# Issuing the second modulation's products directly behind the first's, and the last rows' squares behind the first features

## The chip, the cores and the metric

The kernel runs on one core of a Trainium2 chip. The metric is the device time of one execution in microseconds, and of a set of executions the median. The engines are named as the profile names them: PE multiplies matrices (PEld is its weight load), DVE and ACT work element by element, POOL is a third such engine, and SP only issues DMA transfers.

## The reference

One layer of a diffusion backbone for 128 context rows and 1024 latent rows of width 1024. What matters here is its head: a conditioning vector gives six modulations, of which the first two (shift and scale) enter the normalised rows ahead of the input projection.

```python
def ada_mods(cond, w_ada_l, b_ada_l):
    m = jax.nn.silu(cond) @ w_ada_l + b_ada_l          # 1024 -> 6 x 1024
    return jnp.split(m.reshape(-1, 1, 6 * D_MODEL), 6, axis=-1)

sh1, sc1, g1, sh2, sc2, g2 = mods
h = rmsnorm(x, norm1_w) * (1 + sc1) + sh1
aq, ak, av, mq, mk, mv, mo, mg = jnp.split(h @ w_in, SPLIT_POINTS, axis=-1)
... # attention head group, mLSTM head group, output projection
x = x + g1 * mix
x = x + g2 * swiglu(rmsnorm(x, norm2_w) * (1 + sc2) + sh2, w_gu, w_down)
```

Context rows use a second conditioning vector, so each modulation is a 1024 x 2 result.

## The kernel before

The 1152 rows are nine blocks of 128, handled in three chunks of three blocks (`x3[c]`, c = 0, 1, 2). The program's first 100 us go through these stages.

1. **Loads.** SP issues the rows of chunks 0 and 1, the four pieces `kraw` of the input projection's key, value and gate columns, then sixteen tiles `ada_w[n][k]` (n = 0 the shift's weights, n = 1 the scale's, eight tiles of 512 KB each; the trace calls them `aw`), and last the rows of chunk 2. After them come the four `iraw` tiles of the query columns and, through `ada_rest`, tiles `a4` (trace: `a`) of the four other modulations; these have three buffers and are asked for again as the products free them.
2. **Rows.** `normalise(c)` squares three blocks on ACT (L355), takes an inverse square root on DVE by a dozen dependent operations on 128x3 numbers (L127 to L133, `rsqrt`), and scales the rows on DVE (L358). `turn(c)` transposes them on PE (L116) into two PSUM banks a block, which ACT (L371) and DVE (L372) copy back.
3. **First two modulations.** `strip_products` (L341) multiplies one weight tile half by the padded silu vector; it uses a 32-column strip of PE, so products with different k run side by side. Of each modulation ACT and DVE copy two `part` tiles (L388) from PSUM, `cols_from_strips` turns them into columns with eight small products (L347), and `modulation` adds the bias on DVE. `kvg.pairs` splits the `kraw` pieces into half-precision pairs on ACT and DVE (L218, L219).
4. **Features.** From both modulations a bound is taken and a power-of-two scale made (L397 to L402, with two small PE products, L116 and L175). `features(c)` then writes each chunk as a high part (ACT, L507) and a low part (DVE, L508 and L137), for eight k tiles.
5. **First projection.** `linear_tok` multiplies chunk by chunk with the key/value/gate pairs, three products for each pair (L483 to L485); ACT (L492, L493) and DVE (L496) take the results out. In chunks 1 and 2 the side work `steps` (absolute maxima of the query weights on ACT, L198, then DVE L200, a PE transpose, DVE L171 and L161 to L164, a PE product L175) and `ada` (the a4 products on PE) is woven in.

The order on each engine is not written out: a scheduler places every instruction by its program position, its dependencies and its priority, and the result is one fixed list for each engine. `hot(n)` raises the priority of what is issued inside it by n. `normalise(2)` stands in the program after the products of chunk 0, and `turn(2)` after those of chunk 1. The rows' results are also taken onward: `norm_rope` normalises and rotates the keys (DVE L666 to L686, POOL L668 and L685) and the new key cache goes out (SP, L694).

## Time and profile before

| | |
|---|---|
| median of 3 runs | 1572.1 us (1570.31 to 1574.45) |
| the profiled execution | 1574.08 us, of which 1572.3 us are its span |
| mean granted clock of PE | 0.979 |
| busy share of the span: PE, DVE, ACT, POOL | 95%, 65%, 49%, 17% |
| chain that ended last: PE, DVE, DMA, ACT | 77%, 11%, 5%, 4% |
| PE busy in the first 20 us, and from 20 to 40, 40 to 60, 60 to 80 | 7.79, 16.64, 15.99, 16.78 us |

A row of a timeline gives the start, the time from the first to the last of the merged instructions, the engine, the line, the operation with its tiles, the number of records, and in brackets how long the engine had been idle and what ended the idle time. PE makes two records of one f32 product with a 512-column output in this trace: sixteen products of a modulation are 32 records. SPq is the queue of SP, where a row is the issue of a DMA and not its transfer.

### The profile page before, as it was taken

The numbers are of one execution on the slowest core, as the hardware profiler recorded it, in microseconds if no ns is written. First come the engines' busy times: TensorE is split into PE (matmuls) and PEld (weight loads), VectorE is DVE, ScalarE is ACT, GpSimd is POOL, SyncE is SP. The second block draws the span as 40 slices with busy tenths as digits, with TensorE's granted clock in tenths as the row PEclk, the third lists the DMA queues.
The fourth block names the chain that finished last, engine by engine and source line by source line (L and its number), as shares of the span: only waits on it lengthen the run. The fifth ranks groups of instructions, "written<-read, shape, count | busy, mean of one in ns | idle before, by whom it ended". The sixth has DMA issues, their size and how long they took to land.

```text
span 1572.3 us, 23397 instructions
## 1 busy us (share of the span) xinstructions
PE 1487.7 (95%) x8539; PEld 1247.3 (79%) x8539; DVE 1022.9 (65%) x2025; ACT 771.8 (49%) x1409; POOL 271.4 (17%) x357
## 2 busy tenths in 40 slices
PE   6899999999999689999999999999999999999996
PEld 3544567676766468898998989989898989999995
DVE  4878554737659576677555677877866585554555
ACT  4754465847656344545432444556552443323332
POOL 0213333322343242100110101000010101001111
PEclk9899999999999799999999999999999999999998
DMA  9664323523556847767555447878763545544441
GB/s 360 186 182 157 97 68 41 121 47 68 114 150 162 265 80 197 184 174 175 154 154 149 147 126 236 195 170 180 179 162 114 168 133 168 161 130 138 143 139 54
DMA packets 387881, 236.91 MB, mean 151 GB/s; under 512 B 170198, under 2 KB 346790, under 8 KB 387766
## 3 DMA queue, kind: packets, MB, share of 16 engines
q1 hardware_dynamic: 385110, 231.84, 54.1%
q10 hardware_dynamic: 2656, 3.58, 1.1%
q8 instruction: 67, 1.10, 0.3%
q14 instruction: 48, 0.39, 0.1%
HBM read 183.79 MB, written 13.26 MB: 125 GB/s over the span
## 4 chain that ended last, share of the span: by engine, by line
PE 77%; DVE 11%; DMA 5%; ACT 4%; issue 2%; SPq 0%; POOL 0%; ACTq 0%; DVEq 0%; POOLq 0%
PE mm L1316 11%; PE mm L1317 11%; PE mm L1315 11%; PE mm L1115 5%; PE mm L1116 5%; PE mm L1117 5%; PE S L1035 3%; PE wi L483 3%; PE wi L485 3%; PE wi L484 3%; PE mm L116 2%; PE mm L1147 1%; PE mm L1148 1%; PE mm L1149 1%; PE po L1060 1%
## 5 line engine op out<-in xcount | busy, mean ns | idle before, releaser
L152 ACT CAST whi<-raw 128x1024 fp32r<-128x1024 f32 (+1 forms) x216 | 222.3, 1029 | 411.0 <-PE mm L1316 156.5
L137 DVE TENSOR_TENSOR wlo<-raw,whi 128x1024 fp32r<-128x1024 f32 (+1 forms) x216 | 260.4, 1206 | 202.9 <-ACT whi L152 202.3
L1316 PE MATMUL mm<-aTl,whi 128*128 128x384 f32 x1056 | 355.7, 337 | 2.7 <-DVE aTl L137 2.7
L1317 PE MATMUL mm<-aTh,wlo 128*128 128x384 f32 x1056 | 354.3, 336 | 0.0
L1315 PE MATMUL mm<-aTh,whi 128*128 128x384 f32 x1056 | 353.3, 336 | 0.0
L137 POOL TENSOR_TENSOR hl<-tn,hl 128x384 fp32r<-128x384 f32 x66 | 84.4, 1279 | 840.0 <-ACT hl L1338 748.3
L1316 PEld LDWEIGHTS mm<-aTl,whi 128*128 128x128 f32 x1056 | 198.5, 188 | 3.9 <-DVE aTl L137 3.3
L1315 PEld LDWEIGHTS mm<-aTh,whi 128*128 128x128 f32 x1056 | 198.1, 188 | 0.6
L1317 PEld LDWEIGHTS mm<-aTh,wlo 128*128 128x128 f32 x1056 | 198.4, 188 | 0.0
L1116 PE MATMUL mm<-wlo,hl 128*128 128x512 f32 x372 | 145.7, 392 | 0.0
L1115 PE MATMUL mm<-whi,hl 128*128 128x512 f32 x372 | 144.3, 392 | 0.0
L1117 PE MATMUL mm<-whi,hl 128*128 128x512 f32 x372 | 143.4, 392 | 0.0
L483 PE MATMUL wi<-ipair,hT 128*128 128x384 f16 (+2 forms) x408 | 135.6, 335 | 1.7 <-ACT hT L507 1.2
L484 PE MATMUL wi<-ipair,hT 128*128 128x384 f16 (+2 forms) x408 | 135.6, 335 | 0.0
L485 PE MATMUL wi<-ipair,hT 128*128 128x384 f16 (+2 forms) x408 | 132.1, 335 | 1.0 <-DVE hT L137 1.0
L1042 DVE SCALAR_TENSOR_TENSOR pl<-pr,st,ph 128x1152 f16<-128x1152 f32 (+1 forms) x72 | 96.0, 1333 | 31.7 <-ACT ph L1041 31.4
L1037 DVE TENSOR_REDUCE st<-S 128x1 f32<-128x1152 f32 (+1 forms) x72 | 88.9, 1235 | 16.3 <-PE S L1035 16.1
L1038 ACT ACTIVATE pr<-S,st 128x1152 f32<-128x1152 f32 (+1 forms) x72 | 81.3, 1130 | 32.4 <-DVE st L1037 29.3
L1041 ACT ACTIVATE ph<-pr,st 128x1152 f16<-128x1152 f32 (+1 forms) x72 | 83.9, 1165 | 23.8 <-DVE st L1040 6.7
L1035 PE MATMUL S<-kst,qT 128*128 128x384 f32 (+1 forms) x400 | 87.6, 349 | 4.8 <-ACT pr L1038 4.8
L1104 DVE TENSOR_TENSOR t<-mm,gl 128x512 f32<-128x512 f32 x102 | 69.1, 687 | 26.2 <-DMA gl<-g_d 11.5
L1117 PEld LDWEIGHTS mm<-whi,hl 128*128 128x128 f32 x372 | 69.9, 188 | 14.2
(375 smaller groups left out, 2538.4 us busy)
## 6 DMA issues: line engine op xcount, KB each, us to landing
raw<-in_w_gu_dram SPq DMA_DIRECT2D x132, 512.0 KB
raw<-in_w_down_dram SPq DMA_DIRECT2D x60, 512.0 KB
a<-in_w_ada_dram SPq DMA_DIRECT2D x24, 512.0 KB
gl<-g_d SPq DMA_DIRECT2D x36, 256.0 KB
aw<-in_w_ada_dram SPq DMA_DIRECT2D x16, 512.0 KB
iraw<-in_w_in_dram SPq DMA_DIRECT2D x32, 256.0 KB
raw<-in_w_out_dram SPq DMA_DIRECT2D x12, 512.0 KB
x<-in_x_sample_dram SPq DMA_DIRECT2D x11, 512.0 KB
```

What stands on the lines that cost most here:

```text
L137: (dve if eng == "dve" else pool).tensor_tensor(out=out, in0=full, in1=hi, op=ALU.subtract)
L152: nc.scalar.copy(hi[:, :n], raw[:, :n])
L483: mm(ps[:, :n], ah, wh[:, k % 2, c0 : c0 + n], start=(k == 0), stop=False)
L484: mm(ps[:, :n], ah, wl[:, k % 2, c0 : c0 + n], start=False, stop=False)
L485: mm(ps[:, :n], al, wh[:, k % 2, c0 : c0 + n], start=False, stop=(k == KD - 1))
L1035: mm(S[:, n, 0:w], qT[:, h, :], kst[kv][:, t, c0 + n * w : c0 + (n + 1) * w], start=(t == 0), stop=(t == 1))
L1115: mm(ps, ah, wh[:, k % 2, :], start=(k == 0), stop=False)
L1116: mm(ps, ah, wl[:, k % 2, :], start=False, stop=False)
L1117: mm(ps, al, wh[:, k % 2, :], start=False, stop=(k == nk - 1))
L1315: mm(ps, wh[:, k, :], th[:, k, :], start=(k == 0), stop=False)
L1316: mm(ps, wh[:, k, :], tl[:, k, :], start=False, stop=False)
L1317: mm(ps, wl[:, k, :], th[:, k, :], start=False, stop=(k == KD - 1))
```

## The change

Two things move, both by order of issue alone. A new construct, `tc.issue_after(instruction)`, holds what is issued inside it behind that instruction in the scheduler's order.

- The four PSUM banks of both modulations are taken at once. All products of modulation 0 come first, then its two `part` copies, and `kvg.pairs` only behind the ACT copy. The products of modulation 1 follow directly: those with k = 0 to 3, then the columns of the shift's first half, the product with k = 4, the columns of its second half, then k = 5 to 7. The scale's columns come last, as before. The columns use banks of the other pool (`bank`), and `part` has four buffers in place of two.
- `features(c)` returns its last ACT instruction. `normalise(2)` is held behind that of `features(0)`, and the products and side work of chunk 1 behind that of `features(1)`.

```diff
-    kvg_pairs = kvg.pairs(1)
-
-    for n, out in ((0, shift1), (1, scale1)):
-        halves = [bankA(), bankA()]
-        for k in range(KD):
-            for j, pe in enumerate(halves):
-                strip_products(pe, k, silp, ada_w[n][k][:, j * 512 : (j + 1) * 512], 2 * j)
-        with hot(300):
-            for j, pe in enumerate(halves):
-                part = p0.tile([P, 512], F32, name=nm("part"), tag="part", bufs=2)
-                (nc.scalar.copy if j == 0 else dve.tensor_copy)(part, pe)
-                cols_from_strips(out, n, j, part, bankA)
+
+    halves = [[bankA(), bankA()] for _ in range(2)]
+
+    def first_products(n, ks):
+        for k in ks:
+            for j, pe in enumerate(halves[n]):
+                last = strip_products(pe, k, silp, ada_w[n][k][:, j * 512 : (j + 1) * 512], 2 * j)
+        return last
+
+    def first_parts(n):
+        parts = [p0.tile([P, 512], F32, name=nm("part"), tag="part", bufs=4) for _ in range(2)]
+        dve.tensor_copy(parts[1], halves[n][1])
+        return parts, nc.scalar.copy(parts[0], halves[n][0]).ins
+
+    first_products(0, range(KD))
+    with hot(300):
+        parts, last = first_parts(0)
+    with tc.issue_after(last):
+        kvg_pairs = kvg.pairs(1)
+    for j, ks in enumerate(((0, 1, 2, 3), (4,))):
+        last = first_products(1, ks).ins
+        with hot(300), tc.issue_after(last):
+            cols_from_strips(shift1, 0, j, parts[j], bank)
+    with hot(300):
+        first_products(1, (5, 6, 7))
+        parts, _ = first_parts(1)
+        for j in range(2):
+            cols_from_strips(scale1, 1, j, parts[j], bank)
...
     for c in range(NCH):
         with hot(100):
-            features(c)
+            last = features(c)
...
         if c > 0:
-            weave(prods, chain(steps, ada), KD, 10)
+            with tc.issue_after(last) if c == 1 else nullcontext():
+                weave(prods, chain(steps, ada), KD, 10)
         else:
             emit(prods)
         if c == 0:
-            normalise(2)
+            with tc.issue_after(last):
+                normalise(2)
```

The first place is PE between the two modulations. `aw_0_7` is the last weight tile of the shift, `aw_1_0` the first and `aw_1_7` the last of the scale; `part` are the copies whose columns L347 makes. Before:

```order
L341 MATMUL wi_366<-aw_0_7_167,silp 32x512
L347 MATMUL wi_385<-strip_sel,part_383 128x2 x4
L347 MATMUL wi_393<-strip_sel,part_391 128x2 x4
L341 MATMUL wi_399<-aw_1_0_169,silp 32x512
L341 MATMUL wi_400<-aw_1_0_169,silp 32x512
L341 MATMUL wi_399<-aw_1_1_171,silp 32x512
```

After, from the fourth tile of the scale on:

```order
L341 MATMUL wi_356<-aw_1_3_175,silp 32x512
L347 MATMUL mm_397<-strip_sel,part_373 128x2 x4
L341 MATMUL wi_355<-aw_1_4_177,silp 32x512
L341 MATMUL wi_356<-aw_1_4_177,silp 32x512
L347 MATMUL mm_405<-strip_sel,part_374 128x2 x4
L341 MATMUL wi_355<-aw_1_5_179,silp 32x512
```

The shift's columns leave the place between the two modulations and stand inside the second one. The last product (`aw_1_7`) and what follows it keep their order.

The second place is DVE behind the features of chunk 1: `hT_440` is their last low part, `ry_627` the inverse square root of chunk 2's rows, `x_2` these rows, `isc_689` and `pv_728` the scale of the query weights, for which PE waits. Before, the operations of the root were spread among the features:

```order
L137 TENSOR_TENSOR hT_440<-full_673,hT_440 128x384
L358 TENSOR_SCALAR x_2_134<-x_2_134,ry_627 128x1024 x3
L200 TENSOR_REDUCE isc_689<-isc_689 128x1
L128 TENSOR_SCALAR rh_1120<-rv_1117 128x2
L129 TENSOR_SCALAR ry_1118<-rh_1120 128x2
L131 TENSOR_TENSOR rt_1119<-ry_1118 128x2
L171 TENSOR_REDUCE pv_728<-mm_726 1x1
```

After, the root begins with the last low part, and the rows `x_2` come out as follows:

```order
L133 TENSOR_SCALAR ry_627<-rt_628,ry_627 128x3
L131 TENSOR_TENSOR rt_1119<-ry_1118 128x2
L358 TENSOR_SCALAR x_2_134<-x_2_134,ry_627 128x1024 x3
L132 TENSOR_SCALAR rt_1119<-rt_1119,rv_1117 128x2
L512 TENSOR_SCALAR G<-mm_677,isc_332,gbias 128x2x4 x2
L512 TENSOR_SCALAR G<-mm_678,isc_332,gbias 128x2x4 x2
L133 TENSOR_SCALAR ry_1118<-rt_1119,ry_1118 128x2
L200 TENSOR_REDUCE isc_689<-isc_689 128x1
L512 TENSOR_SCALAR G<-mm_679,isc_332,gbias 128x2x4 x2
L171 TENSOR_REDUCE pv_728<-mm_726 1x1
L685 TENSOR_REDUCE nrs_1181<-nr_143_1179 128x8
L161 TENSOR_SCALAR pv_728<-pv_728 1x1
```

The twelve steps of the root and its three row scalings now stand in one piece ahead of L200 and L171, and a reduction of 128x512 numbers (L685, before L666) stands between L171 and L161.

The third place is PE in the turn of chunk 2: `mm_802` to `mm_831` are its six transposed half blocks, `a_89` to `a_93` the first four `a4` tiles (three buffers, so `a_93` is loaded into that of `a_89`). Before:

```order
L341 MATMUL mm_770<-a_91_759,silp_473 32x256 x4
L116 MATMUL mm_807<-ident,x_2_134 128x128 x4
L116 MATMUL mm_814<-ident,x_2_134 128x128 x4
L116 MATMUL mm_819<-ident,x_2_134 128x128 x4
L341 MATMUL mm_770<-a_93_784,silp_473 32x256 x4
L116 MATMUL mm_826<-ident,x_2_134 128x128 x4
L116 MATMUL mm_831<-ident,x_2_134 128x128 x4
```

After:

```order
L116 MATMUL mm_814<-ident,x_2_134 128x128 x4
L341 MATMUL mm_770<-a_91_759,silp_473 32x256 x3
L341 MATMUL mm_770<-a_93_784,silp_473 32x256 x3
L116 MATMUL mm_819<-ident,x_2_134 128x128 x4
L341 MATMUL mm_770<-a_93_784,silp_473 32x256
L116 MATMUL mm_826<-ident,x_2_134 128x128 x4
L116 MATMUL mm_831<-ident,x_2_134 128x128 x4
```

The products of `a_93`, and with them the wait for its load, now stand ahead of three half blocks in place of two. On ACT the three squares of chunk 2 (L355) leave the place ahead of the first feature: two now stand directly behind the last feature of chunk 1, the third among the results of chunk 0. On SP the output of the key cache (L694) comes ahead of three `a4` loads instead of behind them, and a query row block (L729) ahead of one later `a4` load. Farther on, a few neighbouring instructions of the attention and mLSTM stages trade places.

More of the change, by code (lines that the diff above doesn't have):

```diff
@@ L1 @@
 import math
-from contextlib import ExitStack
+from contextlib import ExitStack, nullcontext
 import concourse.bass as bass
@@ L340, in strip_products @@
         s = (k + turn) % 4
-        mm(ps[32 * s : 32 * s + 32, :], silp[:, k, :], rows, start=(k < 4), stop=(k >= 4), tile_position=(0, 32 * s))
+        return mm(ps[32 * s : 32 * s + 32, :], silp[:, k, :], rows, start=(k < 4), stop=(k >= 4), tile_position=(0, 32 * s))
     def cols_from_strips(out, n, j, part, new):
@@ L506, in features @@
                 s, t = scale1[:, k, cnd : cnd + 1], shift1[:, k, cnd : cnd + 1]
-                act(hh[:, k, i : i + n], v[:, k, i : i + n], AF.Identity, scale=s, bias=t)
+                last = act(hh[:, k, i : i + n], v[:, k, i : i + n], AF.Identity, scale=s, bias=t)
                 dve.tensor_scalar(out=full[:, i : i + n], in0=v[:, k, i : i + n], scalar1=s, scalar2=t, op0=ALU.mult, op1=ALU.add)
             sub(hl[:, k], full, hh[:, k], "dve")
+        return last.ins
     for c in range(NCH):
         with hot(100):
-            features(c)
+            last = features(c)
         prods = linear_tok(kvg_pairs, 0, 272, evac_kvg, (tuple(range(c * CB, c * CB + CB)),), bank if c == 1 else bankA)
         if c > 0:
-            weave(prods, chain(steps, ada), KD, 10)
+            with tc.issue_after(last) if c == 1 else nullcontext():
+                weave(prods, chain(steps, ada), KD, 10)
         else:
```

## The prediction

> **What bounds the kernel now.** I read the page's shares and its chain first, then the first 140 us engine by engine.

> ```profile
> PE 1487.7 (95%) x8539; PEld 1247.3 (79%) x8539; DVE 1022.9 (65%) x2025; ACT 771.8 (49%) x1409; POOL 271.4 (17%) x357
> PE 77%; DVE 11%; DMA 5%; ACT 4%; issue 2%; SPq 0%; POOL 0%; ACTq 0%; DVEq 0%; POOLq 0%
> ```

> PE is idle for 1572.3 - 1487.7 = 85 us in all, and the change works on the part of that in the head. PE's timeline there:

> ```profile
> 26.45 1.25 PE L341 MATMUL wi<-aw,silp 128*32 128x512 f32 x8
> 29.95 3.57 PE L347 MATMUL wi<-strip_sel,part 128*128 128x2 f32 x16 [2.25 <-ACT part L388]
> 33.45 5.41 PE L341 MATMUL wi<-aw,silp 128*32 128x512 f32 x32
> 39.91 1.95 PE L347 MATMUL wi<-strip_sel,part 128*128 128x2 f32 x16 [1.05 <-ACT part L388]
> ```

> The shift's products end at 27.70. PE waits 2.25 us for a copy that stands behind four pair pieces on ACT, makes columns for 3.5 us, and starts the scale's products at 33.45. They end at 38.86. That gap is what the change fills; what it is worth depends on when the scale's weights land. Three views tell: PE's weight loads (timeline), SP's queue (timeline), and the windows of one microsecond, whose last three columns are the granted clock, the DMA share and GB/s.

> ```profile
> 37.80 0.14 PEld L341 LDWEIGHTS wi<-aw,silp 128*32 128x32 f32 x4 [0.33 <-DMA aw<-in_w_ada_dram]
> ```
> ```profile
> 37.77 0.37 SPq L193 DMA_DIRECT2D iraw<-in_w_in_dram  x1
> ```
> ```profile
> 29.00:30.00 1.00, 0.06 (x1) 0.06 (x1) 1.00 (x3) 0.89 (x2) 0.00 (x0) 0.65 1.02 410
> 35.00:36.00 1.00, 1.00 (x8) 0.19 (x4) 0.00 (x0) 0.00 (x0) 0.00 (x0) 0.50 1.01 401
> 37.00:38.00 1.00, 1.00 (x14) 0.30 (x8) 0.00 (x0) 0.00 (x0) 0.00 (x0) 1.00 1.01 406
> ```

> The last weight tile is already waited for: its weight load at 37.80 was held 0.33 us by the DMA. SP's next query load goes out at 37.77, at the same moment. The DMA engines are full (share 1.0, 400 to 410 GB/s), and 0.524 MB at 406 GB/s is one tile in 1.29 us. So the head is bound by the loads, and PE, half-clocked as it was, caught up with them just at the end.

> **The products and columns (part one).** SP's queue keeps its order through all head loads, so the last tile still lands at 37.8. Its product and all behind it (copies, the scale's columns, the bound, the features) keep their order and their lengths. The two columns moved between the products take about half of 1.95 us each at full clock, in pauses between tiles. From 27.8 to 37.8 is 10 us. A tile is four records, so the eight tiles' 32 records take 5.0 us by the first row (8 records in 1.25) and 2.3 by the window from 37 (14 in 1.00); with the 1.95 that is 7.0 us at most, and it fits. ACT's pairs now start behind the copy, about a microsecond later, and their products are not needed before 45, when the first feature starts (row below). This part is worth 0. Its bounds: nothing below, since no product can precede its load; above, what a half clock at 37.8 would cost. At full clock the last tile's product took 38.86 - 37.80 = 1.06, at half it would take 1.06 more, and the columns 3.57 in place of 1.95: +2.7 us in all.

> PE's clock showed 0.65 in the microsecond from 29 to 30, inside a pause of 2.25 us, 0.50 until after 35, and 1.00 at 37. [...]

> **The squares (part two).** ACT before the features, and DVE inside them:

> ```profile
> 39.75 1.06 ACT L355 ACTIVATE jk<-x 128x1024 bf16<-128x1024 f32 x1
> ...
> 43.44 0.63 ACT L198 ACTIVATE jkw<-iraw 128x512 bf16<-128x512 f32 x1 [0.46 <-DMA iraw<-in_w_in_dram]
> 45.16 11.96 ACT L507 ACTIVATE hT<-x,shift,scale 128x128 f16<-128x128 f32 x24 [1.00 <-DVE shift L402]
> ```
> ```profile
> 9.83 0.17 DVE L127 TENSOR_SCALAR rv<-ssx 128x3 f32<-128x3 f32 x1 [2.95 <-ACT jk L355]
> ...
> 12.27 2.08 DVE L358 TENSOR_SCALAR x<-x,ry 128x1024 f32<-128x1024 f32 x3
> ...
> 50.78 0.17 DVE L131 TENSOR_TENSOR rt<-ry 128x3 f32<-128x3 f32 x1
> 50.85 0.68 DVE L508 TENSOR_SCALAR full<-x,scale,shift 128x128 f32<-128x128 f32 x2
> ```

> The squares filled a pause: ACT waits 1.00 us for the shift afterwards, so taking them away gains nothing there. On DVE a step of the root costs 0.07 between independent work (50.78 to 50.85); eleven steps leave the features, -0.8. Alone, the root runs as a dependent chain from 9.83 to 12.27: 2.44. So DVE gains 0.8 and pays 2.44 later. What is late next is the wait chain behind the features of chunk 1:

> ```profile
> 65.27 0.56 DVE L137 TENSOR_TENSOR hT<-full,hT 128x384 f16<-128x384 f32 x1
> 65.74 2.08 DVE L358 TENSOR_SCALAR x<-x,ry 128x1024 f32<-128x1024 f32 x3
> 67.72 0.16 DVE L200 TENSOR_REDUCE isc<-isc 128x1 f32<-128x8 f32 x1
> ...
> 68.28 0.27 DVE L171 TENSOR_REDUCE pv<-mm 1x1 f32<-1x128 f32 x1
> ...
> 69.40 0.13 DVE L164 TENSOR_SCALAR pv<-pv 1x1 f32<-1x1 f32 x1
> ...
> 70.08 0.68 DVE L666 TENSOR_REDUCE nrs<-nr 128x8 f32<-128x512 f32 x1
> ```
> ```profile
> 67.94 0.27 PE L116 MATMUL mm<-ident,isc 128*1 128x128 f32 x1 [1.03 <-DVE isc L200]
> 69.59 0.38 PE L175 MATMUL mm<-pv,one 1*128 1x2 f32 x2 [1.38 <-DVE pv L164]
> ```

> PE stood idle for L200 and L164. In the new order: the last low part ends about 1.1 earlier (the 0.8, and some results of chunk 0 that now stand behind it), at 64.6; root 2.44, so the row scalings start at 67.0 for 65.74 and end at 69.0. Then three or four small operations (0.7 by the pitch of this place), L200 at 69.7, L171 0.56 later at 70.3, the reduction of 0.6 that was behind L175 and now lies in front of L161, and the last four steps with others between them, 0.8: PE's L175 at 71.8 in place of 69.59, **+2.2**. ACT comes out at the same place: the third square (1.06) and a half sum (0.63) now delay the results of chunk 1 and the input of that reduction.

> **The a4 loads and chunk 2.** Behind L175 stand the a4 products and the turn of chunk 2:

> ```profile
> 75.03 0.64 PE L341 MATMUL mm<-a,silp 128*32 128x256 f32 x8
> ...
> 82.84 0.64 PE L341 MATMUL mm<-a,silp 128*32 128x256 f32 x8 [1.68 <-DMA a<-in_w_ada_dram]
> ...
> 135.15 1.09 PE L116 MATMUL mm<-ident,kall 128*128 128x128 f32 x4 [3.64 <-DVE ry L133]
> ```
> ```profile
> 70.72 3.30 SPq L423 DMA_DIRECT2D a<-in_w_ada_dram  x3
> ```
> ```profile
> 77.34 2.41 DVE L508 TENSOR_SCALAR full<-x,scale,shift 128x384 f32<-128x384 f32 x4
> 79.66 0.35 DVE L679 TENSOR_TENSOR nr<-kall,ss 128x64 f32<-128x64 f32 x2
> ...
> 80.52 0.88 DVE L679 TENSOR_TENSOR nr<-kall,ss 128x64 f32<-128x64 f32 x6
> ...
> 84.45 0.69 DVE L686 TENSOR_TENSOR kall<-kall,nr 128x512 f32<-128x512 f32 x1
> ```
> ```profile
> 85.02 1.15 ACT L218 ACTIVATE ipair<-iraw,isc 128x1024 f16<-128x1024 f32 x1 [0.88 <-PE wi L485]
> ```
> ```profile
> 87.24 1.21 DVE ipair L219
> 88.45 0.02 issue
> 88.47 0.37 SPq L193
> ```

> The fourth a4 tile was asked for at 70.72 and used at 75.03: 4.3 us at most. Asked for at 72.9 it comes by 77.2, and three half blocks now queue behind it on PE, so the features of chunk 2 start near 79.9 for 77.34, +2.5. The output of the key cache, put ahead of these loads on SP, is ready before 72.9, so it costs nothing. DVE gets part back: the rotation products (0.35 + 0.88) and the sum after them (0.61 to the next start, 85.06; I take 0.6) are now done before, -1.8. But the pair piece at 87.24 also needs ACT's half, which was ready at 85.02 + 1.15 = 86.17, a slack of 1.1, and that half follows PE's products, 2.5 late. So the piece starts 2.5 - 1.1 = 1.4 later, near 88.7, and the query-side load at 88.47 goes out **+1.5** later. From there all is one chain into PE (PE's wait of 3.64 us at 135.15 is for DVE at its end), so a shift passes to the end. Bounds: 0, if that slack takes it, to +2.5.

> **Sum.** 0 (part one) + 1.5 (part two) = +1.5: 1574.08 (span 1572.3 and 1.8 around it) becomes 1575.6. The profiled execution is 2.0 above the median of 1572.1, so the forecast in medians is 1573.6. Below 0.3%, 4.7 us, a measurement of this kernel tells little from no change.

> **Rivals.**

> *The half clock (slower).* Place: the scale's last product and columns, and the turn of chunk 2, where PE now waits 4.9 us for L175 (67.94 - 1.03 = 66.9 to 71.8; before, to 69.59, 2.7). It decides where PE, fed a tile every 1.29 us, is granted 0.5 at 37.8. Price: +2.7 there, +1.7 for a second half-clocked spell of 3.4 us, +1.5: +5.9, 1578.0. For it: the clock fell in 2.25 us of pause. Against it: PE has work for most of the 10 us. Chance 0.31.

> *Nothing passes.* The 1.1 of slack on ACT is larger than I read it, or later waits take the 1.5: 1572.1. For it: 85 us of idle PE lie ahead. Against: the chain is unbroken at 88 us. Chance 0.14.

> *The gap closes (faster).* If the tiles land earlier than PE's wait shows, the products and two columns run on from 27.7 at full clock, 3.6 (between 2.3 and 5.0) + 1.95 = 5.6 us, to 33.3 in place of 38.86: -5.6, 1566.5, where the later delay is absorbed. For it: the wait at 37.80 is only 0.33 us, and the scheduler's earlier work may leave more slack than one row shows. Against: 400 GB/s at a share of 1.0. Chance 0.20.

> **How the numbers follow.** The forecast has 0.35, with a range of its own from 1572.1 to 1574.6 by the bounds 0 and +2.5. It and the second rival (0.14) lie within 0.3%, with 0.04 of the first rival and 0.03 of the last: 0.56. Slower is the rest of the half clock: 0.27. Faster is the rest of the last: 0.17. The range goes from 1566.0 to 1579.0; it leaves out the lower half of the spread about the last rival's 1566.5 and the upper part of the first one's.

> **What would show it.** Right: PE's weight loads of the scale each wait for the DMA, the last near 37.8; the first feature at about 45; L175 near 71.8 and the features of chunk 2 near 80. Wrong: the last product before 37, a clock of 0.5 at 38, or L175 at 70 or before.

## The result, and the profile after

| | before | after |
|---|---|---|
| median | 1571.6 us (6 runs, 1570.3 to 1574.5) | 1577.8 us (6 runs, 1576.0 to 1581.6) |
| ratio | | 1.0036, 95% interval 1.0026 to 1.0046 |
| profiled execution, span | 1574.08, 1572.3 | 1576.94, 1575.1 |

The change made the kernel 6.2 us slower, 0.36%. The two profiled executions are only 2.9 us apart: the one of before lies 2.5 above its kernel's median, the one of after 0.9 below its own. The page of after, busy times and the chain that ended last:

```profile
PE 1493.1 (95%) x8539; PEld 1248.7 (79%) x8539; DVE 1022.1 (65%) x2025; ACT 770.2 (49%) x1409; POOL 273.6 (17%) x357
PE 78%; DVE 9%; DMA 5%; ACT 4%; issue 2%; POOL 1%; SPq 1%; ACTq 0%; DVEq 0%; POOLq 0%
```

PE does the same 8539 instructions and is busy 5.4 us longer, while its idle time fell from 84.6 to 82.0. So in these two executions the loss shows as products that ran slower, not as more waiting.

**The head.** PE's timeline of after at the end of the scale, with its columns, and two windows of a microsecond (columns as before: the last three are granted clock, DMA share, GB/s):

```profile
36.91 1.05 PE L341 MATMUL wi<-aw,silp 128*32 128x512 f32 x4 [0.23 <-DMA aw<-in_w_ada_dram]
38.63 2.66 PE L347 MATMUL mm<-strip_sel,part 128*128 128x2 f32 x16 [0.67 <-ACT part L390]
```
```profile
39.00:40.00 1.00, 1.00 (x10) 1.00 (x9) 0.25 (x2) 0.00 (x0) 0.00 (x0) 0.83 1.07 399
40.00:41.00 1.00, 1.00 (x7) 1.00 (x6) 0.09 (x1) 0.00 (x0) 0.00 (x0) 0.50 1.03 396
```
```profile
44.85 11.91 ACT L523 ACTIVATE hT<-x,shift,scale 128x128 f16<-128x128 f32 x24 [6.27 <-DVE shift L418]
```

The gap between the two modulations is gone, and nothing came of it: the last tile's product still waits for its load. In this execution the head loads came 0.7 to 0.9 us earlier (SP's `kraw` entries start at 6.55 for 7.23, its `aw` entries at 12.53 for 13.46, the last tile is there at 36.91 for 37.80); the change does not touch SP's order there. From the last tile to the first feature it is 44.85 - 36.91 = 7.94 us, before it was 45.16 - 37.80 = 7.36: 0.6 longer. The clock fell to 0.5 during the columns, which took 2.66 us for 1.95.

**Chunk 2.** DVE and PE of after behind the features of chunk 1:

```profile
65.03 2.08 DVE L358 TENSOR_SCALAR x<-x,ry 128x1024 f32<-128x1024 f32 x3
...
68.11 0.16 DVE L200 TENSOR_REDUCE isc<-isc 128x1 f32<-128x8 f32 x1 [0.18 <-ACT jkw L198]
...
79.35 2.41 DVE L524 TENSOR_SCALAR full<-x,scale,shift 128x384 f32<-128x384 f32 x4
...
90.07 1.28 DVE L219 SCALAR_TENSOR_TENSOR ipair<-iraw,isc,ipair 128x1024 f16<-128x1024 f32 x1 [2.60 <-ACT ipair L218]
```
```profile
70.50 0.55 PE L175 MATMUL mm<-pv,one 1*128 1x2 f32 x2 [1.90 <-DVE ry L129]
...
83.19 0.64 PE L341 MATMUL mm<-a,silp 128*32 128x256 f32 x8 [1.87 <-DMA a<-in_w_ada_dram]
...
84.93 1.08 PE L341 MATMUL mm<-a,silp 128*32 128x256 f32 x8 [1.11 <-DMA a<-in_w_ada_dram]
```

L175 is 0.9 later than before, the features of chunk 2 are 2.0 later, and the pair piece 2.9 later. SP's queue and ACT's half of the pair piece say how the last step came:

```profile
72.12 12.13 SPq L439 DMA_DIRECT2D a<-in_w_ada_dram  x7
...
91.38 1.19 SPq L193 DMA_DIRECT2D iraw<-in_w_in_dram  x2
```
```profile
88.89 1.15 ACT L218 ACTIVATE ipair<-iraw,isc 128x1024 f16<-128x1024 f32 x1 [2.22 <-PE wi L501]
```

The chain of after between 66 and 100 us (start, length, what) runs through one a4 load and then through PE:

```profile
79.28 0.87 PE mm L466
80.17 4.72 DMA a<-in_w_ada_dram
84.93 1.08 PE mm L341 x8
86.02 0.79 PE wi L501 x3
```

And the windows, first of before, then of after:

```profile
82.00:92.00 10.00, 9.16 (x76) 6.83 (x77) 9.86 (x16) 4.39 (x5) 2.46 (x2) 1.00 0.68 205
```
```profile
82.00:92.00 10.00, 7.71 (x48) 4.60 (x49) 7.40 (x14) 3.55 (x6) 0.00 (x0) 0.66 0.65 208
```

PE waits 3.0 us for two a4 tiles, its clock is at half from 84.0 to 90.9 us (0.66 in the mean of the window, 3.4 us of full-speed time), and it gets through 48 products in place of 76. ACT waits for those products with its half of the pair piece, DVE for ACT, and the query-side load for DVE. Two rows of three products, first of before, then of after, tell the wait from the clock; ACT's half starts at the end of the second row:

```profile
83.42 0.52 PE L485 MATMUL wi<-ipair,hT 128*128 128x272 f16 x3
84.47 0.51 PE L485 MATMUL wi<-ipair,hT 128*128 128x272 f16 x3
```
```profile
85.95 0.86 PE L501 MATMUL wi<-ipair,hT 128*128 128x272 f16 x3
87.96 0.89 PE L501 MATMUL wi<-ipair,hT 128*128 128x272 f16 x3
```

Behind the last a4 tile PE is 2.5 us late (85.95 for 83.42), at the end of the second row 3.9 (88.85 for 84.98). So 1.4 us of the delay at this place came from the half clock.

Around 100 us like instructions are 3.8 us late on SP and DVE and 4.6 on PE. In these two executions the delay does not stay so: on PE it is 2.4 us from 180 to 300 us, 0.1 to 0.4 from 380 to 540, and 2.9 from 650 us on. Its larger steps down lie where only the execution of before has a half-clocked spell (at 165.8 and 374.1 us), its rise where only that of after has one (572.1 and 613.1).

### The profile page after: what moved, and what is told of

Its sections match the earlier page's. It is cut to its first block, busy times and chain, and to the rows that moved or that the text cites. A ratio compares the mean times of both kernels' runs of the same rounds, so it can differ in the third digit from the quotient of the medians.

```text
span 1575.1 us, 23404 instructions
## 1 busy us (share of the span) xinstructions
PE 1493.1 (95%) x8539; PEld 1248.7 (79%) x8539; DVE 1022.1 (65%) x2025; ACT 770.2 (49%) x1409; POOL 273.6 (17%) x357
## 4 chain that ended last, share of the span: by engine, by line
PE 78%; DVE 9%; DMA 5%; ACT 4%; issue 2%; POOL 1%; SPq 1%; ACTq 0%; DVEq 0%; POOLq 0%
PE mm L1335 11%; PE mm L1336 11%; PE mm L1334 11%; PE mm L1134 5%; PE mm L1135 5%; PE mm L1136 5%; PE S L1054 4%; PE wi L501 3%; PE wi L499 3%; PE wi L500 3%; PE mm L1166 2%; PE mm L1167 2%; PE mm L1168 1%; DMA aw<-in_w_ada_dram 1%; PE po L1079 1%
## 5 line engine op out<-in xcount | busy, mean ns | idle before, releaser
L137 DVE TENSOR_TENSOR wlo<-raw,whi 128x1024 fp32r<-128x1024 f32 (+1 forms) x216 | 260.5, 1206 | 201.7 <-ACT whi L152 198.8
L137 POOL TENSOR_TENSOR hl<-tn,hl 128x384 fp32r<-128x384 f32 x66 | 84.0, 1272 | 841.0 <-ACT hl L1357 728.8
L1061 DVE SCALAR_TENSOR_TENSOR pl<-pr,st,ph 128x1152 f16<-128x1152 f32 (+1 forms) x72 | 94.1, 1307 | 32.4 <-ACT ph L1060 32.1
L1056 DVE TENSOR_REDUCE st<-S 128x1 f32<-128x1152 f32 (+1 forms) x72 | 88.8, 1233 | 12.6 <-PE S L1054 11.4
```

Source lines behind the costliest of these rows:

```text
L137: (dve if eng == "dve" else pool).tensor_tensor(out=out, in0=full, in1=hi, op=ALU.subtract)
```

## The experiments

Each was timed beside the kernel before, whose median in these comparisons was 1571.7 (first four), 1570.8 (next four), 1572.6 (next three) and 1571.3 (last). "Wait" is PE's wait for a4 tiles between 66 and 92 us, "query load" the issue of the first query-side load, both from the profile.

| run | median | ratio (95%) | wait | query load |
|---|---|---|---|---|
| before | 1571.6 | | 2.7 | 88.5 |
| after | 1577.8 | 1.0026 to 1.0046 | 3.0 | 91.4 |
| e1 products only | 1580.9 | 1.0037 to 1.0070 | 5.8 | 96.7 |
| e2 squares only | 1577.9 | 1.0020 to 1.0049 | 5.5 | 96.2 |
| e3 after, four a4 | 1579.6 | 1.0034 to 1.0063 | 0.0 | 90.3 |
| e4 after, root free | 1577.1 | 1.0022 to 1.0043 | 2.5 | 89.7 |
| e5 before, four a4 | 1576.3 | 1.0017 to 1.0051 | 1.5 | 86.8 |
| e6 before, rows twice | 1577.9 | 1.0020 to 1.0050 | 2.9 | 93.7 |
| e7 after, fewer a4 | 1582.6 | 1.0056 to 1.0083 | 3.3 | 92.9 |
| e8 before, fewer a4 | 1578.2 | 1.0026 to 1.0052 | 3.9 | 88.1 |
| e9 after, filled | 1573.4 | 1.0000 to 1.0021 | 2.5 | 88.8 |
| e10 before, filled | 1577.4 | 1.0019 to 1.0046 | 5.0 | 90.8 |
| e11 before, four a4, hot | 1584.9 | 1.0071 to 1.0098 | 0.5 | 88.3 |
| e12 root free, filled | 1575.1 | 1.0013 to 1.0036 | 4.1 | 89.7 |

### Each part alone (e1, e2)

```diff
 e1: the kernel after
-            with tc.issue_after(last) if c == 1 else nullcontext():
-                weave(prods, chain(steps, ada), KD, 10)
+            weave(prods, chain(steps, ada), KD, 10)
-            with tc.issue_after(last):
-                normalise(2)
+            normalise(2)
 e2: the kernel before, with these two holds
```

> The change's first part alone: products and columns as in the kernel after, normalise(2) and the work of chunk 1 not held. The scheduler then puts the twelve steps of chunk 2's root and its three row scalings on DVE into the bound's chain, between L171 and L164. Theory A (the loss is the second part: DVE is late for chunk 2, the a4 loads are asked for late, PE starves and its clock halves near 84 us): the features start about 2 us later than the 44.9 of the kernel after, chunk 2 is not late, no half clock between 82 and 92; median 1571 to 1574. Theory B (the loss is the first part: PE's pauses between the scale's tiles halve its clock at 39 us): the clock is 0.5 from 39 us on as in the kernel after, median 1576 to 1579.

> The change's second part alone: normalise(2) held behind the features of chunk 0, the work of chunk 1 behind those of chunk 1; products and columns as before. Theory A: L175 near 71, the features of chunk 2 near 80, PE waits 2 to 3 us in all for a4 tiles at 82 to 86 and the clock is 0.5 for at least 3.4 us after; median 1576 to 1578. Theory B: 1571 to 1573.5, by the 1.5 us at most that pass from DVE.

Either part alone is slower, but e1 does not isolate the first part. DVE and PE of e1:

```profile
45.03 0.28 DVE L171 TENSOR_REDUCE pv<-mm 1x1 f32<-1x128 f32 x1
45.23 2.06 DVE L358 TENSOR_SCALAR x<-x,ry 128x1024 f32<-128x1024 f32 x3
47.63 0.13 DVE L164 TENSOR_SCALAR pv<-pv 1x1 f32<-1x1 f32 x1
```
```profile
50.89 0.41 PE L499 MATMUL wi<-ipair,hT 128*128 128x272 f16 x1 [2.42 <-ACT hT L523]
```

Without the hold the row scalings of chunk 2 land inside the bound's chain, and the first product of the projection is 5 us later than before (45.71), more than the 2 expected. That is what the hold of the second part is for, and so e1 does not show what the first part costs by itself. In e2 the second part by itself makes the kernel as slow as the whole change does (1577.9 and 1577.8), as theory A said. L175 comes at 71.69 and the features of chunk 2 at 81.65. PE's timeline, and SP's queue:

```profile
84.85 0.64 PE L341 MATMUL mm<-a,silp 128*32 128x256 f32 x8 [1.23 <-DMA a<-in_w_ada_dram]
89.72 1.08 PE L341 MATMUL mm<-a,silp 128*32 128x256 f32 x8 [4.23 <-DMA a<-in_w_ada_dram]
```
```profile
96.17 1.21 SPq L193 DMA_DIRECT2D iraw<-in_w_in_dram  x2
```

The waits for a4 tiles are 5.5 us, more than the 2 to 3 of theory A, the clock is at half from 70.7 to 77.5 and from 87.8 to 94.6 us, and the query-side load is 7.7 us late. That is 4.8 later than in the kernel after, at the same median: the time does not follow this load one to one.

### More DVE work at the same place (e6)

```diff
             dve.tensor_scalar(out=x3[c][:, i], ..., scalar1=rs[:, i : i + 1], ...)
+            if c == 2:
+                dve.tensor_scalar(out=x3[c][:, i], in0=x3[c][:, i], scalar1=1.0, ...)
```

> The kernel before with each of the three row scalings of chunk 2 followed by one more operation of the same length on the same rows (a product with 1.0, which changes nothing): DVE gets about 2.0 us more work in front of L200. Theory E (a delay of this place passes to the end one to one): median +1.7 to +2.3, 1573.5 to 1574. Theory F (it is made larger by the a4 loads that go out later, and by the half clock behind PE's longer waits): +4 to +6, 1575.5 to 1577.5, with PE waiting 5 us for a4 tiles in place of 2.7. Theory G (it is absorbed): 1572.

This run sizes a delay at this place without the change. DVE and PE of e6 (L360 is the added operation, L668 the reduction that is L666 in the kernel before):

```profile
68.06 0.15 DVE L200 TENSOR_REDUCE isc<-isc 128x1 f32<-128x8 f32 x1
...
68.20 1.89 DVE L360 TENSOR_SCALAR x<-x 128x1024 f32<-128x1024 f32 x3
...
70.07 0.27 DVE L171 TENSOR_REDUCE pv<-mm 1x1 f32<-1x128 f32 x1
...
71.20 0.66 DVE L668 TENSOR_REDUCE nrs<-nr 128x8 f32<-128x512 f32 x1
```
```profile
72.32 0.58 PE L175 MATMUL mm<-pv,one 1*128 1x2 f32 x2 [3.78 <-DVE pv L164]
```

The 1.9 us of added work stand behind L200 and ahead of L171, not in front of L200 as expected, and the scheduler also put the reduction ahead of L162 to L164, as it did in the kernel after. So it is not a pure delay of 2.0 us: L175 is 2.7 us late (72.32 for 69.59), the features of chunk 2 are 4.5 late (81.81 for 77.34), the query-side load 5.2 (93.66 for 88.47), and the median 7.2 (5.5 by the ratio, interval 3.1 to 7.9 us). Windows of e6:

```profile
66.00:82.00 16.00, 11.19 (x79) 6.26 (x78) 12.66 (x60) 7.32 (x15) 3.22 (x5) 0.79 0.36 104
82.00:92.00 10.00, 7.14 (x54) 3.65 (x53) 7.93 (x15) 5.70 (x10) 0.00 (x0) 0.83 0.83 259
```

Before, the clock was 0.89 and 1.00 in these stretches. 16 x 0.10 + 10 x 0.17 = 3.3 us of clock are lost on top of the 2.7; the sum is 6.0, of which 5.2 reached the load. Of the two causes in theory F the half clock fits: the wait for a4 tiles was 2.9 us, not the 5 I expected. All executions together say the same. One minus the mean granted clock, times the span, is 32.4 us in the mean of e6 and 27.0 in that of the kernel before beside it; the 5.4 between them are as much as the mean times differ by (5.3). In e2 it is 33.1 for 28.0, with mean times 5.8 apart.

### Taking the waits away (e3, e5, e7, e8, e11)

```diff
 e3 (after), e5 (before):
-    def ada_rest(ns, silp, new_a4, new_part, new_row, early=2):
+    def ada_rest(ns, silp, new_a4, new_part, new_row, early=3):
-    ... tag="a4", bufs=3),
+    ... tag="a4", bufs=4),
 e7 (after), e8 (before):
-    weave(prods, chain(steps, ada), KD, 10)
+    weave(prods, chain(steps, ada), KD, 10 if c == 1 else 6)
 e11: e5, and in linear_tok
-            for ps, b in zip(banks, grp):
-                evac(b, ps)
+            with hot(200):
+                for ps, b in zip(banks, grp):
+                    evac(b, ps)
```

> The kernel after with four buffers for the a4 tiles and a lookahead of three, so that the fourth tile is loaded near 44 us and later tiles one use earlier. Theory A2 (most of the loss is the wait for a4 tiles at 82 to 86 and the half clock behind it): no half clock between 84 and 92, the first query-side load near 89 in place of 91.4; median 1573 to 1575. Theory A1 (the loss is DVE's delay alone, which passes on whatever PE's clock does): the load stays near 91 and the median at 1577 to 1578.

> The kernel before with four a4 buffers and a lookahead of three. In the kernel before PE waited 2.7 us for a4 tiles between 66 and 100 us. Theory C (these waits lie on the path that sets the end): the waits go, median 1568 to 1570. Theory D (what is gained there is given back at the next wait behind it, as with the same edit on the kernel after, whose time did not fall): 1571 to 1573.

> The kernel after with six in place of ten units of side work woven into the products of chunk 2, so that the a4 products that waited for their loads at 82 to 86 us stand later. Theory A2 (that wait and the half clock behind it are most of the loss): no wait for an a4 tile and no half clock between 82 and 92, median 1573 to 1575. Theory D: 1576 to 1579, the wait comes back where the a4 products stand now.

> The same edit on the kernel before: six in place of ten units of side work in chunk 2. It shows what the edit costs or gains by itself, without the change: by theory C 1569 to 1571, by theory D 1571.5 to 1574. The difference between this run and the last one is the change's loss without the wait for a4 tiles in chunk 2.

> The kernel before with four a4 buffers, a lookahead of three and a higher priority for the results of the first projection, so that one half tile of query maxima fewer stands on ACT ahead of the results of chunk 2, on which PE waited 2.8 us at 95 us with four buffers alone. Theory D, with its place right (ACT's wait for the query loads in front of these results gave back what the fourth buffer had gained): PE's wait at 95 us at most 2, median 1 to 2 us below the 1576.3 of four buffers alone, 1574 to 1575.5. If the wait shrinks and the median stays at 1576 to 1577, the loss of these variants lies behind 100 us.

All five missed the gain that theories A2 and C spoke of. Fewer units of side work (e7, e8) only moved the a4 products; PE waited 3.3 and 3.9 us for their tiles. With that edit in both kernels the change costs 4.4 us (e7 against e8). e8 issues the query-side load 0.4 us earlier than before, has no half-clocked spell between 52 and 137 us, and is 7.4 us slower all the same, so its loss lies behind 100 us.

A fourth buffer did what it should in chunk 2 (no wait at all in e3, the query-side load 1.7 us earlier in e5), and the time did not follow. In e3 the half clock did not go with the wait: it stood at 67.6 to 77.9 us, as long as both spells of after between 66 and 92 us together. So e3 is no test of that half of theory A2. In e5 PE's timeline shows the next wait:

```profile
95.09 0.38 PE L483 MATMUL wi<-ipair,hT 128*128 128x512 f16 x1 [2.83 <-ACT vall L493]
```

ACT takes out the results of chunk 2 only behind the maxima of the next query weights, for whose loads it waits; PE arrived earlier and stood, and its clock was at half from 95.3 to 98.8 us. Around 100 us e5 is 1.5 us behind before on PE, between 240 and 440 us 3 to 4, and 1.4 at the end of these two executions. In e11 that wait shrank (1.86 us in place of 2.83), yet the kernel lost 10 us between 440 and 560 us, half of them in longer half-clocked spells. Its median lies above everything I expected; the loss of that variant lies behind 100 us.

Laid side by side, PE's order behind 100 us differs from that of the kernel it was made of in 1500 to 2200 instructions in each of these five runs, in the attention and mLSTM stages above all; in after, e2 and e6 it differs from that of before in 32 to 35. Which of those moves cost what was not tried; so e3 and e5 show only that the price stayed when the a4 wait went, and e2 and e6 are the cleaner tests.

### The root free (e4)

```diff
         if c == 0:
-            with tc.issue_after(last):
-                normalise(2)
+            ssx2 = squares(2)
+            with tc.issue_after(bound_used):      # the last operation of the bound
+                normalise(2, ssx2)
```

> The kernel after, with the second part's hold on normalise(2) cut down: the three squares are free (ACT's pause ahead of the features), the root and the row scalings are held only behind the bound's last operation. DVE's order then has the root's steps among the features again and L200 ahead of the row scalings. Theory A: L175 at 69.5 or before, features of chunk 2 at 77.5 or before, no half clock between 84 and 92; median 1570 to 1572.5. Theory B: 1576 or more, since the first part is as in the kernel after.

(`squares` is the first half of `normalise`, in a function of its own.) More than half of the delay at the query-side load went: 89.67, no half clock between 82 and 92, and PE 1.9 us late at 100 us in place of 4.6. But L175 came at 70.45, not 69.5, the features of chunk 2 at 79.7, not 77.5, the spell of half clock behind L175 lasted to 77.2 us in place of 73.8, and the median stayed near that of after. In this execution another spell fell on the scale's products. Windows of e4 (the clock is 0.50 from 38 to 39 us too):

```profile
36.00:37.00 1.00, 1.00 (x8) 0.00 (x1) 0.23 (x2) 0.00 (x0) 0.00 (x0) 0.60 1.03 410
37.00:38.00 1.00, 1.00 (x8) 0.19 (x4) 0.00 (x0) 0.00 (x0) 0.00 (x0) 0.50 1.00 397
```

So the price that the first rival named at 37.8 us exists, in some executions; here on the products alone, for the columns took 1.95 us as before.

### PE kept in work (e9, e10, e12)

```diff
         ps = bank()
+        for _ in range(fill):
+            mm(ps[:, 0:P], ident, ident, start=True, stop=True)
         mm(ps[:, 0:2], one, v[:, 2:4], start=True, stop=True)
```

The count is 5 in e9 (kernel after), 3 in e10 (before) and 3 in e12 (the kernel of e4). The scheduler then also moves two or three tiles' a4 products ahead of L175, so these runs change more than PE's idle time.

> The kernel after with five small products (128x128, results overwritten by the product of L175) queued on PE ahead of L175. With them in its count the scheduler also puts the products of the first two a4 tiles ahead of L175, where PE stood idle for 1.6 and 1.9 us. Theory F (the loss is made of a4 loads that go out late and of PE's half clock behind its idle time): the a4 loads go out near 70.5 in place of 72.1, less clock is lost between 66 and 92 us than the 5.0 us of the kernel after, the first query-side load goes out before 90; median 1573 to 1576. Theory D (what is gained at one wait is given back at the next): median 1577 to 1579, with the wait named by the profile behind 92 us.

> The kernel before with three such products, so that the products of the first three a4 tiles stand ahead of L175. Theory F: the a4 waits of 2.7 us and the half clock at 70 to 74 us shrink, median 1568 to 1571. Theory D: 1572 to 1577, as for every other edit of this stretch so far, also those that took work or waits away.

> The kernel after with the root of chunk 2 free (as in the run with that edit alone, 1577.1) and three small products queued on PE ahead of L175, so that the products of the first three a4 tiles stand ahead of L175 too. Theory F (late a4 loads and PE's half clock behind its idle time): the a4 loads go out at 70 or before, in place of 72.1 in either of the two kernels it is made of, little clock is lost between 66 and 92 us, the first query-side load goes out near 88; median 1569.5 to 1573, at or below the kernel before. Theory D (a gain there is given back behind 100 us): 1574 to 1577.

e9 keeps the whole change and is 0.8 us slower than before by the medians, 1.6 by the ratio, where the change cost 6.2 and 5.7. PE's timeline of e9 between 81 and 85 us, and its window:

```profile
81.38 0.64 PE L343 MATMUL mm<-a,silp 128*32 128x256 f32 x8 [0.73 <-DMA a<-in_w_ada_dram]
...
84.00 0.64 PE L343 MATMUL mm<-a,silp 128*32 128x256 f32 x8 [1.18 <-DMA a<-in_w_ada_dram]
```
```profile
82.00:92.00 10.00, 8.82 (x77) 6.48 (x75) 9.28 (x17) 5.37 (x8) 0.00 (x0) 1.00 0.79 249
```

The two waits are 1.9 us together in place of 3.0, the clock stays at 1.00, PE does 77 products in place of 48, and the query-side load goes out at 88.8, although the features of chunk 2 start no earlier than in after (79.48 and 79.35). One point of the expectation missed: the first a4 load still went out at 72.12; the seventh came nearly 2 us earlier. e10 is the counter-example on the kernel before. The same filler made PE reach the a4 tiles early, and it waited 5.0 us for them:

```profile
82.00:92.00 10.00, 7.99 (x54) 5.16 (x53) 8.24 (x14) 3.35 (x4) 2.43 (x2) 0.68 0.48 152
```

The half clock that before has from 70 to 74 us stands there from 81.6 to 88.5, and the kernel became 4.8 us slower. e12, e4 with the filler, lies between e4 and e9, as theory D said: the first a4 load went out at 71.59, the query-side load at 89.74. It has no half clock at all between 54 and 118 us and is still 3.9 us slower than before, so the clock of this stretch is not the whole price. No version tried beats before, and e9 comes to within 1.6 us of it (interval 0 to 3.3).

## Why the prediction was right or wrong

The measured 1577.8 lies outside the forecast's own range of 1572.1 to 1574.6. The wide range holds it only because the half clock's price had been taken into it.

**Part one at 0: right for the products, short by 0.6 for what follows.** The last tile's product waits for its load as it did (that it came before 37, a sign set for being wrong, is due to the loads of this execution, 0.9 us earlier), and the features' start moved by the 0.6 us that the half-clocked columns cost in this execution. The bound of +2.7 held. That PE would have its full clock at 37.8 us, as the 0 takes it, was an estimate: after was granted 1.00 up to 39.66, the execution of e4 0.50 from 37 to 39.

**L175 and the features of chunk 2: right in the sum, with luck in the terms.** Forecast 71.8 and 79.9. Measured 70.50 and 79.35, in an execution whose loads came 0.9 us earlier, so 71.4 and 80.2 on the scale of before. The place of the reduction L685 and of the a4 tile in front of three half blocks was as the order said. But the last low part started 3.3 us earlier than before (61.93 for 65.27) where 1.1 was forecast, and it was ACT, delayed by the squares, and not DVE's root for which L200 waited at the end (0.18 us, at 68.11).

**From there to the query-side load: the step that failed.** I let ACT's half follow PE's products 2.5 us late and took 1.1 us of slack off, to +1.5. The load came out at +2.9 (91.38 for 88.47), +3.8 with the earlier loads counted. The slack held as read: ACT's half started 3.9 us later (88.89 for 85.02) and the pair piece 2.9. The term that failed is PE's products, 3.9 late at that place in place of 2.5; the 1.4 between are the half clock, for PE ran at 0.66 between 82 and 92 us, where it ran at 1.00 before. e6 shows it without the change: +2.7 at L175 becomes +5.2 here, with 3.3 of clock lost on the way. e9 shows the reverse: with the clock at 1.00 the load is back at 88.8, although DVE's root stands where the change put it.

**The half clock: the rival that came true, at another place.** Its time, 1578.0, is near the measured 1577.8, but it was made of 2.7 at 37.8 us and 1.7 behind L175. In the profile of after the first was 0.6 and the second nothing (0.89 between 66 and 82 us in both kernels, with one spell each, 70.26 to 73.67 before and 70.39 to 73.80 after; the 1.7 is half of such a length, 3.41), and 3.4 us lay at 84 to 91 us, behind the a4 waits, which I had priced for their own length only; 1.4 of them reached the query-side load. That its time is near the measured one is luck. The place behind L175 is real in other kernels: the spell there is 6.8 us long in e2, e4, e6 and e7, where before and after have 3.4. I gave it 0.31 against 0.35 for the forecast; the words against it ("PE has work for most of the 10 us") speak of the first place alone.

**Nothing passes: wrong, and one to one also wrong.** The delay was 3.8 to 4.6 us at 100 us, at most 0.4 from 380 to 540 us, and 2.9 at the end of these two executions, so the last is not the first carried through; the medians are 6.2 apart. Part of that is clock again: one minus the mean granted clock, times the span, is 28.03 us in the mean of 20 executions of before (those beside e1 to e4) and 31.26 in the six of after, so 3.2 us of 6.0 in the means. Where the rest arises is open.

**The gap closes: wrong,** for the reason given there: the loads fill their engines until 37 us, in after with 393 to 422 GB/s at a share of 0.98 to 1.05 in each microsecond from 20 on.

## What to carry to other kernels

Where an engine's clock falls with its idle time, as PE's does in these traces (0.50 from 84.04 to 90.86 us in after, whose waits of 1.87 and 1.11 us end at 83.19 and 84.93), price each new wait twice, by its length and by a slow spell behind it, and take slack off only then. Added work at the place in question (e6) measures this in one run; look at where the scheduler put it before calling it a plain delay. And taking away the wait for the a4 tiles (e3, e5) made neither kernel faster: look first at what the engine meets next when it arrives earlier.

## What was not expected of the hardware

```profile
29.30:36.13 6.83, 6.18 (x32) 4.20 (x36) 2.21 (x6) 0.59 (x2) 0.00 (x0) 0.50 1.03 408
36.13:42.95 6.82, 4.91 (x41) 2.49 (x33) 1.77 (x8) 3.68 (x7) 0.00 (x0) 1.00 1.02 397
42.95:53.19 10.24, 7.09 (x31) 4.38 (x31) 9.64 (x42) 8.79 (x21) 0.00 (x0) 0.50 1.07 316
53.19:70.26 17.07, 14.66 (x129) 11.82 (x130) 16.97 (x56) 12.77 (x36) 6.61 (x6) 1.00 0.16 35
70.26:73.67 3.41, 3.41 (x29) 1.30 (x19) 2.11 (x14) 2.72 (x3) 0.87 (x2) 0.50 0.48 153
```
```profile
39.66:53.32 13.66, 9.55 (x43) 6.19 (x42) 10.80 (x42) 8.47 (x19) 0.61 (x1) 0.50 1.08 327
53.32:70.39 17.07, 13.64 (x116) 11.14 (x114) 16.48 (x67) 15.67 (x42) 8.56 (x8) 1.00 0.10 23
70.39:73.80 3.41, 3.30 (x23) 2.05 (x24) 1.95 (x16) 2.19 (x2) 1.04 (x1) 0.50 0.12 24
73.80:84.04 10.24, 8.16 (x69) 3.86 (x67) 8.24 (x21) 7.24 (x12) 1.32 (x2) 1.00 0.84 263
84.04:90.86 6.82, 5.93 (x30) 3.50 (x31) 4.22 (x8) 1.73 (x2) 0.00 (x0) 0.50 0.67 212
```

In each of the 14 traces the spells behind 20 us (but for the last, which runs into the end of the kernel) last whole multiples of the 3.41 us measured here, from 3.4 to 20.5, and start whole multiples of 3.41 us apart: in before at 29.30, 42.95 and 70.26 us, 13.65 and 27.31 apart, 4 and 8 steps. Where the grid lies differs from execution to execution: a spell starts at 70.26 us in before, at 70.39 in after and at 70.7 in e2. In these traces the length of a wait alone does not tell whether a spell follows; the share of the step ahead in which PE was busy tells more. The step ahead of 84 us, first in before, then in after:

```profile
80.50:83.91 3.41, 1.71 (x21) 0.74 (x22) 3.41 (x13) 1.69 (x4) 2.37 (x1) 1.00 0.90 279
```
```profile
80.63:84.04 3.41, 1.33 (x14) 0.50 (x12) 3.41 (x7) 3.19 (x6) 0.00 (x0) 1.00 0.86 264
```

Busy for 0.50 of the step, PE kept its clock; busy for 0.39, it lost half of it. From 60 to 1540 us of all the traces, each of the 72 full-clocked steps with a busy share under 0.44 was followed by a half-clocked one, 17 of 73 between 0.44 and 0.55, and 5 of 5751 above; before and after alone have 14 of 14, 3 of 12 and none of 815. Between 36 and 44 us, where the columns are, shares of 0.47 to 0.74 were followed by one as well (0.64 from 39.54 in before, 0.74 from 36.25 in after). Waits for a4 tiles of 1.7 (before), 2.0 (e8) and 2.2 us (e4) were followed by none; 1.8 us in e10, and 1.9 and 1.1 with a short stretch of work between in after, were followed by 6.8 us at 0.5. The execution of e4 had such a spell on the scale's products; that of after, with the same order there, had one 3.5 us later. The mean granted clock of single executions of the kernel before ranged from 0.980 to 0.988 in 20 of them, with times from 1569.7 to 1576.1 us.
